# Where two engines' loop code is placed, and which engine opens the section: a streaming row-variance kernel on one Trainium2 core

## The chip, the core and the metric

The kernel runs on one core of one Trainium2 chip. The metric is the device time of one execution in microseconds (us); less is better. Of the core's engines four take part: SyncE (SP in the profile), which issues every transfer; VectorE (DVE) and ScalarE (ACT), which do the arithmetic; and GpSimd (POOL), which copies small results. TensorE (PE) runs only the barriers.

## The reference

For every row of 1,024 numbers the variance is wanted, as the mean of the squares less the square of the mean:

```python
def reference(x):                     # x: 32 x 512 x 1024, float32
    mean_sq = np.mean(x**2, axis=-1)
    sq_mean = np.mean(x, axis=-1)**2
    return (mean_sq - sq_mean).astype(np.float32)   # 32 x 512
```

There are 16,384 rows, 64 MiB in all, and each number is read once.

## The kernel before, in words

The rows are laid out as 128 partitions by 128 columns; a column is one row of 1,024 numbers in each of the 128 partitions. The columns go by in groups of eight (`GROUP`), and one load brings a group, 4 MiB, from `in_x_dram` into one of three buffers `xt0`, `xt1`, `xt2` (`NBUF`). Twelve groups go through the buffers in four turns (`TURNS`) of three. The last 32 columns are loaded by smaller and smaller transfers (`END_LOADS`: 8, 6, 6, 4, 3, 2, 1 columns, and four half columns): the first of these goes into `xt0` once more, the others into `xt_end`.

Of each group of eight, ACT takes three columns (`NACT`) and DVE five. ACT makes a column in two passes over it: `act_mean` (L104) sums it into `neg_mean`, `act_var` (L109) sums the squares of the difference. DVE makes a column with two `bn_stats` (one for each half, L100) and one `bn_aggr` (L163). What they find for a turn stands in `stage`, and POOL copies the variances from there to `mv` (L146), which is stored at the end by two transfers. The end columns are written straight to `mv` (L175 to L199 on DVE, L104 and L109 on ACT).

The order of the work is written by hand, with semaphores, inside one critical section (`tc.tile_critical`, L123), in which nothing is scheduled by a planner. `load` (L82) adds 16 to a buffer's `landed` semaphore when it has landed, one for each of 16 DMA engines. `take` (L96) waits for a semaphore and takes the same number off it again. DVE, once a buffer has landed, adds one to `go` for ACT; ACT adds one to `act_done`; and DVE's last `bn_aggr` of a group adds one to `done`, on which SP waits before it loads that buffer again. All loads stand in one queue, SP's, one after the other.

The four turns are a loop in the program of DVE (L150) and one in the program of ACT (L205), each made by `nc.Fori`. Its argument `head_slot` fixes where in the engine's program the loop's first instruction stands: at slot 128 (`HEAD`) of a block of 256 instruction slots (`FETCH_BLOCK_INSTRUCTIONS`). It does so with an alignment instruction just ahead of the loop, which the program loader turns into a branch over the padding:

```python
            self.engines[e].addr_align(
                FETCH_BLOCK_INSTRUCTIONS, offset=slot, max_nops=0
            )
        self.br(loop_start, engines=engines)
```

In the trace this branch is the compare-and-branch record of L150 on DVE and of L205 on ACT. ACT also loads its function table (L204) ahead of its loop.

Around the section stand instructions that are not in the kernel's text. First comes a barrier of all engines (L257): each adds one to a gather semaphore, POOL waits for them all and then releases all. Then the section is opened by one engine, its synchronizing engine, here SP: it adds one to a semaphore by a no-operation, and each of SP, POOL, DVE and ACT waits for that in a branch into the section. At its end the same engine, SP, adds one to a second semaphore; SP, POOL, DVE and ACT wait for it and report back, SP waits for the reports and adds once more to the first one, and SP goes on to a barrier (L268) by way of a drain that waits for this. A second barrier ends the program. With `no_gpsimd_drain=True` POOL reports by a no-operation in place of a drain.

Of the kernel before, what the change touches and what calls it, by code (L numbers as in the profile page):

```python
# [7 lines left out]


# [1 line left out]
def kernel(  # L11
# [13 lines left out]
    nc = tc.nc  # L25
# [3 lines left out]
    ENG = mybir.EngineType  # L29
# [13 lines left out]
    TURNS = 4  # L43
# [6 lines left out]
    HEAD = 128  # L50
# [14 lines left out]
    sync, act, dve, gps = nc.sync, nc.scalar, nc.vector, nc.gpsimd  # L65
# [12 lines left out]
    def load(dst, c0, n, sem, f0=0, f=D):  # L78
        b0, pitch, row0 = next(b for b in BLOCKS if b[0] <= c0 < b[0] + b[1])
        assert c0 + n <= b0 + pitch  # L80
        ap = [[pitch * D, P], [D, n], [1, f]] if n > 1 else [[pitch * D, P], [1, f]]
        sync.dma_start(  # L82
            out=dst,
            in_=dataclasses.replace(xf, offset=(row0 + c0 - b0) * D + f0, ap=ap),
        ).then_inc(sem, 16)

    def store(block):
        b0, pitch, row0 = block
        sync.dma_start(
            out=dataclasses.replace(out, offset=row0, ap=[[pitch, P], [1, pitch]]),  # L90
            in_=mv[:, 1, b0 : b0 + pitch],
        ).then_inc(stored, 16)

    def take(engine, sem, n):
        engine.wait_ge(sem, n)
        engine.sem_inc(sem, -n)  # L96

    def halves(st, xcol):
        for h in range(2):
            last = dve.bn_stats(out=st[:, h, :], in_=xcol[:, h * H : (h + 1) * H])  # L100
        return last

    def act_mean(i, xcol, nm):
        return act.activation(  # L104
            out=junk[i], in_=xcol, func=ACTF.Copy, scale=-S / D, accum_out=nm
        )

    def act_var(i, xcol, nm, var):
        return act.activation(  # L109
            out=junk_sq[i], in_=xcol, func=ACTF.Square, scale=S, bias=nm, accum_out=var  # L110
        )
# [8 lines left out]
        at += n  # L120
    assert at == ncols - IN_HALVES

    with tc.tile_critical(no_gpsimd_drain=True):  # L123

        for g in range(TURNS * NBUF):
            if g >= NBUF:
                sync.wait_ge(done, g - NBUF + 1)
            load(xt[g % NBUF], g * GROUP, GROUP, landed[g % NBUF])
        sync.wait_ge(done, TURNS * NBUF - NBUF + 1)
        load(xt[0], END0, GROUP, landed_end[0])  # L130
        c = END0 + GROUP
        for b, n in enumerate(END_LOADS[1:], 1):
            k = c - END0 - GROUP
            load(xt_end[:, k : k + n, :] if n > 1 else xt_end[:, k, :], c, n, landed_end[b])
            c += n
        b = len(END_LOADS)
        for c in range(c, ncols):
            for h in range(2):
                dst = xt_end[:, c - END0 - GROUP, h * H : (h + 1) * H]
                load(dst, c, 1, landed_end[b], h * H, H)  # L140
                b += 1

        gps.sem_inc(copied, 1)
        for t in range(TURNS):
            gps.wait_ge(done, (t + 1) * NBUF)
            gps.tensor_copy(  # L146
                out=mv[:, 1, t * PER_TURN : (t + 1) * PER_TURN], in_=stage[:, :, 1]
            ).then_inc(copied, 1)

        with nc.Fori(0, TURNS, engines=[ENG.DVE], head_slot={ENG.DVE: HEAD}):  # L150
            take(dve, copied, 1)
            for b in range(NBUF):
                take(dve, landed[b], 16)
                dve.sem_inc(go, 1)
                mine = range(b * GROUP + NACT, (b + 1) * GROUP)
                for j in mine:
                    last = halves(stats[:, j, :, :], xt[b][:, j - b * GROUP, :])
                last.then_inc(dve_step, 1)
                take(dve, dve_step, 1)
                for j in mine:  # L160
                    if j == mine[-1]:
                        take(dve, act_done, 1)
                    last = dve.bn_aggr(out=stage[:, j, :], in_=stats[:, j, :, :])  # L163
                last.then_inc(done, 1)
        n = 0
        waiting = None
        seen = -1
        for b, c, col in end_cols:
            if END_WHO[c - END0] != "D":
                continue  # L170
            if b != seen:
                dve.wait_ge(landed_end[b], 16)
                seen = b
            st = stats_end[:, c - END0, :, :]
            dve.bn_stats(out=st[:, 0, :], in_=col[:, :H])  # L175
            if waiting:
                waiting()
            n += 1
            dve.bn_stats(out=st[:, 1, :], in_=col[:, H:]).then_inc(dve_step, 1)  # L179

            def waiting(n=n, c=c, st=st):
                dve.wait_ge(dve_step, n)
                dve.bn_aggr(out=mv[:, :, c], in_=st)  # L183

        b = len(END_LOADS)
        for c in range(ncols - IN_HALVES, ncols):
            st = stats_end[:, c - END0, :, :]
            col = xt_end[:, c - END0 - GROUP, :]
            dve.wait_ge(landed_end[b], 16)
            dve.bn_stats(out=st[:, 0, :], in_=col[:, :H])  # L190
            waiting()
            dve.wait_ge(landed_end[b + 1], 16)
            n += 1
            dve.bn_stats(out=st[:, 1, :], in_=col[:, H:]).then_inc(dve_step, 1)  # L194
            b += 2

            def waiting(n=n, c=c, st=st):
                dve.wait_ge(dve_step, n)
                return dve.bn_aggr(out=mv[:, :, c], in_=st)  # L199

        waiting().then_inc(dve_step, 1)
        dve_steps = n + 1

        act.preload_act_table(ACTF.Square)  # L204
        with nc.Fori(0, TURNS, engines=[ENG.Activation], head_slot={ENG.Activation: HEAD}):  # L205
            for b in range(NBUF):
                take(act, go, 1)
                mine = range(b * GROUP, b * GROUP + NACT)
                for i, j in enumerate(mine):
                    last = act_mean(i, xt[b][:, i, :], neg_mean[:, j : j + 1])  # L210
                last.then_inc(act_step, 1)
                take(act, act_step, 1)
                for i, j in enumerate(mine):
                    last = act_var(i, xt[b][:, i, :], neg_mean[:, j : j + 1], stage[:, j, 1:2])
                last.then_inc(act_done, 1)
        n = 0
        for b in range(len(END_LOADS)):
            mine = [(c, col) for bb, c, col in end_cols if bb == b and END_WHO[c - END0] == "A"]
            if not mine:
                continue  # L220
            act.wait_ge(landed_end[b], 16)
            for i, (c, col) in enumerate(mine):
                k = c - END0
                last = act_mean(i, col, neg_mean_end[:, k : k + 1])
            n += 1
            last.then_inc(act_step, 1)
            act.wait_ge(act_step, n)
            for i, (c, col) in enumerate(mine):
                k = c - END0
                last = act_var(i, col, neg_mean_end[:, k : k + 1], mv[:, 1, c : c + 1])  # L230
            n += 1
            last.then_inc(act_step, 1)
        act_steps = n

        sync.wait_ge(copied, 1)
        store(BLOCKS[0])
        sync.wait_ge(act_step, act_steps)
        sync.wait_ge(dve_step, dve_steps)
        store(BLOCKS[1])
        sync.sem_clear(range(sems[0].num, sems[-1].num + 1))  # L240
        sync.wait_ge(stored, 32)
        sync.sem_clear(stored)
# [30 lines left out]
```

## Time and profile before

| | before |
|---|---|
| median of 3 runs (lowest to highest) | 165.64 us (165.6 to 165.7) |
| time of the profiled execution | 165.63 us |
| its span in the profile | 163.7 us, so 1.9 us lie outside |
| DVE busy | 107.0 us, 65% of the span |
| ACT busy | 107.3 us, 66% |
| POOL busy | 1.0 us, 1% |
| DMA queue q1 (the loads and stores) | 67.18 MB, 96.2% of 16 DMA engines |
| DMA queue q14 (instructions) | 2 packets, 0.02 MB |
| read from HBM | 67.11 MB, 410 GB/s over the span |

The span runs from the first to the last recorded instruction of the kernel. The share of q1 says how much of the time of all 16 DMA engines its packets filled. A busy share of an engine is a mean over the whole span; DVE and ACT have nothing to do until the first load has landed, and the profile shows their first column at 13.94 and 13.98 us.

### The profile page before, as it was taken

The numbers are of one execution on the slowest core, as the hardware profiler recorded it, in microseconds if no ns is written. First come the engines' busy times: TensorE is split into PE (matmuls) and PEld (weight loads), VectorE is DVE, ScalarE is ACT, GpSimd is POOL, SyncE is SP. The second block draws the span as 40 slices with busy tenths as digits, with TensorE's granted clock in tenths as the row PEclk, the third lists the DMA queues.
The fourth block names the chain that finished last, engine by engine and source line by source line (L and its number), as shares of the span: only waits on it lengthen the run. The fifth ranks groups of instructions, "written<-read, shape, count | busy, mean of one in ns | idle before, by whom it ended". The sixth has DMA issues, their size and how long they took to land. (4 is left out here: it accounts for less than half of the span.)

```text
span 163.7 us, 615 instructions
## 1 busy us (share of the span) xinstructions
DVE 107.0 (65%) x243; ACT 107.3 (66%) x189; POOL 1.0 (1%) x8
## 2 busy tenths in 40 slices
DVE  0005929487492957839296692948749397859993
ACT  3005939488493957939397593948849398759692
POOL 0000000000000000000000000000000000000000
DMA  6999999999998999999999989999999999999980
GB/s 204 432 400 480 400 424 472 392 488 400 408 488 384 440 456 392 480 408 400 480 400 424 472 384 464 432 400 480 400 408 488 406 396 468 396 430 412 405 297 14
DMA packets 3602, 67.19 MB, mean 411 GB/s; under 512 B 656, under 2 KB 656, under 8 KB 1296
## 3 DMA queue, kind: packets, MB, share of 16 engines
q1 hardware_dynamic: 3600, 67.18, 96.2%
q14 instruction: 2, 0.02, 0.0%
HBM read 67.11 MB, written 0.07 MB: 410 GB/s over the span
## 5 line engine op out<-in xcount | busy, mean ns | idle before, releaser
L100 DVE BATCH_NORM_STATS2 stats<-xt 128x6 f32<-128x512 f32 x120 | 72.4, 679 | 41.1 <-DVEq L96 41.1
L104 ACT ACTIVATE junk<-xt 128x1024 bf16<-128x1024 f32 x39 | 40.7, 1045 | 45.9 <-ACTq L96 43.3
L109 ACT ACTIVATE junk_sq<-xt,neg_mean 128x1024 f32<-128x1024 f32 x36 | 39.7, 1104 | 1.5
L163 DVE BATCH_NORM_AGGREGATE stage<-stats 128x2 f32<-128x12 f32 x60 | 7.6, 177 | 6.9 <-DVEq L96 5.2
L104 ACT ACTIVATE junk<-xt_end 128x1024 bf16<-128x1024 f32 x8 | 8.4, 1050 | 4.9 <-DMA xt_end<-in_x_dram 4.8
L175 DVE BATCH_NORM_STATS2 stats_end<-xt_end 128x6 f32<-128x512 f32 x14 | 9.5, 679 | 3.2 <-DMA xt_end<-in_x_dram 3.2
L109 ACT ACTIVATE junk_sq<-xt_end,neg_mean_end 128x1024 f32<-128x1024 f32 x8 | 8.9, 1113 | 0.2
L179 DVE BATCH_NORM_STATS2 stats_end<-xt_end 128x6 f32<-128x512 f32 x14 | 9.0, 640 | 0.0
L104 ACT ACTIVATION_READ_ACCUMULATOR junk<-xt 128x1 f32 x39 | 7.2, 186 | 0.0
L109 ACT ACTIVATION_READ_ACCUMULATOR junk_sq<-xt,neg_mean 128x1 f32 x36 | 6.7, 186 | 0.0
L175 DVE BATCH_NORM_STATS2 stats_end<-xt 128x6 f32<-128x512 f32 x5 | 3.4, 681 | 2.3 <-DMA xt<-in_x_dram 2.3
L183 DVE BATCH_NORM_AGGREGATE mv<-stats_end 128x2 f32<-128x12 f32 x19 | 3.7, 194 | 0.0
L109 ACT ACTIVATE junk_sq<-xt,neg_mean_end 128x1024 f32<-128x1024 f32 x3 | 3.3, 1104 | 0.0
L179 DVE BATCH_NORM_STATS2 stats_end<-xt 128x6 f32<-128x512 f32 x5 | 3.2, 648 | 0.0
L204 ACT ACT_TABLE_LOAD x1 | 1.3, 1283 | 0.9 <-SPq L123 0.9
L190 DVE BATCH_NORM_STATS2 stats_end<-xt_end 128x6 f32<-128x512 f32 x2 | 1.4, 695 | 0.4 <-DMA xt_end<-in_x_dram 0.4
L146 POOL COPY mv<-stage 128x24 f32<-128x24 f32 x4 | 0.8, 204 | 127.0 <-DVE stage L163 127.0
L109 ACT ACTIVATION_READ_ACCUMULATOR junk_sq<-xt_end,neg_mean_end 128x1 f32 x8 | 1.5, 186 | 0.0
L104 ACT ACTIVATION_READ_ACCUMULATOR junk<-xt_end 128x1 f32 x8 | 1.5, 186 | 0.0
L194 DVE BATCH_NORM_STATS2 stats_end<-xt_end 128x6 f32<-128x512 f32 x2 | 1.3, 650 | 0.0
L109 ACT ACTIVATION_READ_ACCUMULATOR junk_sq<-xt,neg_mean_end 128x1 f32 x3 | 0.6, 186 | 0.0
L199 DVE BATCH_NORM_AGGREGATE mv<-stats_end 128x2 f32<-128x12 f32 x2 | 0.4, 202 | 0.0
(4 smaller groups left out, 0.4 us busy)
## 6 DMA issues: line engine op xcount, KB each, us to landing
xt<-in_x_dram SPq DMA_DIRECT2D x13, 4096.0 KB, 21.6
xt_end<-in_x_dram SPq DMA_DIRECT2D x2, 3072.0 KB, 32.0
xt_end<-in_x_dram SPq DMA_DIRECT2D x1, 2048.0 KB, 39.8
xt_end<-in_x_dram SPq DMA_DIRECT2D x1, 1536.0 KB, 43.1
xt_end<-in_x_dram SPq DMA_DIRECT2D x1, 1024.0 KB, 45.1
xt_end<-in_x_dram SPq DMA_DIRECT2D x4, 256.0 KB, 42.0
xt_end<-in_x_dram SPq DMA_DIRECT2D x1, 512.0 KB, 45.9
out_dram<-mv SPq DMA_DIRECT2D x1, 56.0 KB, 1.6
```

The lines of the kernel that those rows point to most:

```text
L100: last = dve.bn_stats(out=st[:, h, :], in_=xcol[:, h * H : (h + 1) * H])
L104: return act.activation(out=junk[i], in_=xcol, func=ACTF.Copy, scale=-S / D, accum_out=nm)
L109: return act.activation(out=junk_sq[i], in_=xcol, func=ACTF.Square, scale=S, bias=nm, accum_out=var)
L146: gps.tensor_copy(out=mv[:, 1, t * PER_TURN : (t + 1) * PER_TURN], in_=stage[:, :, 1]).then_inc(copied, 1)
L163: last = dve.bn_aggr(out=stage[:, j, :], in_=stats[:, j, :, :])
L175: dve.bn_stats(out=st[:, 0, :], in_=col[:, :H])
L179: dve.bn_stats(out=st[:, 1, :], in_=col[:, H:]).then_inc(dve_step, 1)
L183: dve.bn_aggr(out=mv[:, :, c], in_=st)
L190: dve.bn_stats(out=st[:, 0, :], in_=col[:, :H])
L194: dve.bn_stats(out=st[:, 1, :], in_=col[:, H:]).then_inc(dve_step, 1)
L199: return dve.bn_aggr(out=mv[:, :, c], in_=st)
L204: act.preload_act_table(ACTF.Square)
```

## The change

`head_slot` is dropped from both loops. In its place the two engines get the same alignment instruction, with the same block and the same offset, ahead of the critical section, so that on DVE and ACT slot 128 is now the first instruction behind that alignment (the waiting branch into the section), and the loops follow a few slots later. The section's synchronizing engine is now GpSimd (`ENG.Pool`) and not SP, so the opening no-operation, the collection of the reports and the closing no-operation are POOL's.

```diff
+from concourse.bass_core_rust import FETCH_BLOCK_INSTRUCTIONS
...
-    with tc.tile_critical(no_gpsimd_drain=True):
+    for engine in (act, dve):
+        engine.addr_align(FETCH_BLOCK_INSTRUCTIONS, offset=HEAD, max_nops=0)
+
+    with tc.tile_critical(sync_engine=ENG.Pool, no_gpsimd_drain=True):
...
-        with nc.Fori(0, TURNS, engines=[ENG.DVE], head_slot={ENG.DVE: HEAD}):
+        with nc.Fori(0, TURNS, engines=[ENG.DVE]):
...
-        with nc.Fori(0, TURNS, engines=[ENG.Activation], head_slot={ENG.Activation: HEAD}):
+        with nc.Fori(0, TURNS, engines=[ENG.Activation]):
```

No transfer, no arithmetic instruction and no semaphore inside the section is changed. The lines of the changed kernel stand one to four further down than those of the kernel before.

## The prediction

> **What bounds the kernel now.** I read the shares first: DVE and ACT are busy 65% and 66%, the load queue 96.2%. The chain of waits then says what ended last (share of the span; DMA, engine or SP's queue, and line):
>
> ```profile
> DMA 28%; DVE 2%; SPq 2%; issue 0%
> ...
> DMA xt_end<-in_x_dram 28%; SPq L82 2%; DVE stats_end L190 1%; DVE stats_end L194 1%; DVE mv L199 0%; DVE stage L163 0%; DVE mv L183 0%
> ```
>
> It reaches back only to 108 us, where the last loads are issued; before that the DMA row of the slices is full from the second slice on, so the transfers set the pace throughout. What an edit outside the loops can move is the beginning, the end, and anything that shares the DMA engines. The timeline's first microseconds (start, duration, engine, line):
>
> ```profile
> 0.34 0.10 POOL L257 MEMSET const-uint8-127<- 128x1 uint8 x1
> 0.91 1.28 ACT L204 ACT_TABLE_LOAD   x1 [0.91 <-SPq L123]
> 0.94 1.34 SPq L82 DMA_DIRECT2D xt<-in_x_dram  x3
> 13.94 2.47 DVE L100 BATCH_NORM_STATS2 stats<-xt 128x6 f32<-128x512 f32 x4 [13.94 <-DVEq L96]
> ```
>
> The first load is issued at 0.94 us, after the opening by SP (L123). DVE computes nothing for 13 us more. The DMA view of two windows, 2 to 3 us and 3.5 to 4.5 us (queue: packets, MB, share of 16 engines), shows what else is on the DMA engines:
>
> ```profile
> q1 hardware_dynamic: 13, 0.43, 145.8%
> q14 instruction: 1, 0.01, 4.3%
> ```
>
> ```profile
> q1 hardware_dynamic: 16, 0.52, 124.5%
> q14 instruction: 1, 0.01, 1.9%
> ```
>
> Two instruction fetches fall into the load stream. 4.3% and 1.9% of 16 engine-microseconds are 0.69 and 0.30 us. The packet records give them in full: 8,192 bytes each, from 2.134 us (0.688) and from 3.911 us (0.307); the first data packets start at 1.975 us. Elsewhere in the span this queue has nothing.
>
> The landing records have 16 increments for each load, one a DMA engine. For the first load 15 come between 12.58 and 13.12 us, the last at 13.71. For the last load 15 come between 158.79 and 159.29, the last at 159.90. So one DMA engine is late by 0.59 to 0.61 us from beginning to end, never catching up, and every wait for a load waits for it. A 32,768-byte packet takes a DMA engine 1.21 us in the steady stream, so 8,192 bytes are a quarter of that, 0.30 us, and two fetches are 0.61 us: the lateness. On the late engine the packet starts fit as well: a data packet starts at 2.819, as the first fetch ends (2.134 + 0.688 = 2.822), another at 4.214, as the second ends (4.218). I read it so: both fetches went to one DMA engine, inside the stream, and the whole kernel runs behind that engine.
>
> The end (timeline of DVE):
>
> ```profile
> 157.96 0.69 DVE L190 BATCH_NORM_STATS2 stats_end<-xt_end 128x6 f32<-128x512 f32 x1 [0.36 <-DMA xt_end<-in_x_dram]
> ...
> 160.67 0.21 DVE L199 BATCH_NORM_AGGREGATE mv<-stats_end 128x2 f32<-128x12 f32 x1
> ```
>
> DVE restarts at 157.96, 0.03 us after a landing at 157.93, and follows landings to the last at 159.90. ACT's last run starts at 156.00 from a landing at 155.97. Both tails move with the landings, unchanged in length.
>
> **The change part by part.**
>
> *Start of the loads.* Before, SP passes the barrier at 0.656, does its opening no-operation at 0.721, the branch that waits for it at 0.791, and issues at 0.944. Afterwards POOL opens: it releases the barrier at 0.614, its next instruction can follow after the 0.077 us between its two barrier records (0.691), and an engine sees it 0.036 us later (SP's no-operation at 0.721, ACT's branch at 0.757). SP branches at about 0.73 in place of 0.791: 0.06 us earlier. This alone moves 15 of the DMA engines.
>
> *The fetches.* Before, the alignment branch runs at 1.001 us on ACT and at 1.048 on DVE, behind the wait for the section, the register move and, on ACT, the issue of the table load. Afterwards it follows the barrier directly, at about 0.66 + 0.065 (SP's step from 0.656 to 0.721): 0.725 on ACT, 0.73 on DVE, 0.28 and 0.32 us earlier. If these branches bring on the fetches, which first show 1.1 us after them, the first starts near 1.83 in place of 2.134, and the loads at 1.975 - 0.06 = 1.91. The late DMA engine then begins its work, the same bytes, about 0.30 us earlier, and ends that much earlier: I take 0.30 us, by the shift of the branch. Bounds: at worst the late engine gains only the 0.06 of the loads (fetches not moved); at best both are through before its data come, and it falls in with the others: 0.59 + 0.06 = 0.65 us.
>
> One rule speaks against any gain here. The Trainium skill, "Runtime: NRT & Kernel Launch", section "Instruction fetch mechanics", has the sequencer fetch ahead of itself, with the cost of crossing a block mostly hidden. For DVE's and ACT's own time the trace agrees, since they wait until 13.9 us; for the DMA engine that carries the fetch it does not, by the 0.6 us lateness. By the page alone this term would be 0.06 us and the total about 165.4 us.
>
> A second one offers another cause of the late engine: "DMA: Bandwidth & Descriptors", section "Latency and other measured facts", finds two of the sixteen engines usually slower. The lateness here is as large at 13 us as at 159, so it is one event at the start and no lower rate. By that page the lateness would stay, and the total again be about 165.4 us.
>
> *What the fetches' cover hides.* DVE's alignment branch takes 0.545 us to its next instruction (1.048 to 1.593). It now comes ahead of the section's wait; with the 0.20 us of that branch (0.778 to 0.980) and the move DVE is at its loop by about 1.55 us, ACT's table load runs from about 1.4 to 2.7. Both then wait for the first landing, 13 us away; without that cover the branch would cost 0.55 us. The loops start two slots further on; their back edge (0.42 us on DVE, three times) falls into idle time: DVE sits 41.1 us ahead of its loop's statistics, ACT 43.3. I cost these edits at nothing.
>
> *The end of the section.* Before, from SP's last clear at 162.551: SP signals at 162.610, POOL answers at 162.652, SP drains at 162.689, collects at 162.763 and 162.822, signals again at 162.888, drains at 162.963 and 163.026, and POOL passes the barrier at 163.058: 0.507 us. Afterwards POOL has signalled the end long before, after its fourth copy, and SP drains where it signalled, at 162.610. Two chains follow. SP's own instructions are two collecting waits and two drains; with the steps they had before (0.074, 0.059, 0.066 and 0.063) SP reports to the barrier at 162.872 and POOL passes 0.032 later, at 162.904. POOL's answer, for which SP's first of these drains waits, comes in time: POOL sees SP's report 0.042 later (162.652), does its closing no-operation after 0.077 (162.729), seen after 0.04 at 162.77, where SP drains at 162.809. So the path is shorter by 163.058 - 162.904 = 0.15 us: one signal of SP's own and one no-operation less. Behind POOL's new waits nothing of its own is queued but the barrier. Bounds: if POOL's three steps took twice as long each, SP's drain would come at 162.93 and 0.03 us would be left; if SP's barrier report followed POOL's answer directly (162.77 + 0.063 + 0.032), it would be 0.19.
>
> *The sum.* 0.30 + 0.15 = 0.45 us (the 0.06 of the loads is inside the 0.30, since the late engine sets the end). The profiled execution took 165.63 us (span 163.7 and 1.9 around it); 165.63 - 0.45 = 165.18, and against the median of 165.64 the same: **165.2 us**, 0.3% less. Bounds: 0.06 + 0.03 = 0.09 (165.5), and 0.65 + 0.19 = 0.84 (164.8).
>
> **The rivals.** *The fetches leave the stream altogether.* Both come together near 1.83, and the late engine's data only after them; a later start of data on some DMA engines (first packets from 1.975 to 2.53 on the others) leaves room. Then the next-latest engine sets the end: 0.65 + 0.15 = 0.80, 164.8 us. Against it: one fetch alone took 0.69 us, two reach 2.4 or later.
>
> *The fetches stay where they are.* They may belong to an engine whose branch doesn't move, since the records don't name the owner. For it: the second comes 2.9 us after the branches. Against it: just two engines branch over padding, just two fetches follow. Then 0.06 + 0.15 = 0.21, 165.4 us, no difference that can be told: about 0.2%, 0.33 us, is what a measurement of this kernel can tell from no change.
>
> *Slower: the end of DVE's program crosses into code that isn't loaded.* Counted from the loop's head at slot 128, DVE's last barrier instruction is at slot 256, the first of the next block; two slots are now pushed in ahead of the loop, so three instructions of the closing barriers lie beyond. If that block had to be fetched then, all engines would wait in the barrier for as long as from a branch to the end of the fetch at the start (1.048 to 2.822): 1.77 - 0.45 = 1.3 us slower, 166.9 us. Against it: DVE's last instruction before ran at 163.623, with SP's at 163.613 and no fetch near; the block was there. It decides only if the block is no longer loaded ahead.
>
> **How the numbers follow.** Forecast 0.45, fetches clear of the stream 0.28, fetches stay 0.18, slower 0.09. Faster by over 0.2% (under 165.31 us): all of the second and most of the first, which has it where its saving passes 0.33, 0.66 together. Within 0.2%: the third and the rest of the first, 0.25. Slower: 0.09. The range runs from 164.7 to 165.5: the bounds of the sum with 0.1 below for the scatter of the runs (165.6 to 165.7); it takes in two rivals and leaves the slow case out.
>
> **What would show it.** First load issue at 0.88 us in place of 0.94; the alignment branches near 0.73; instruction packets starting at or before 1.9 us; the gap between the last and the last but one landing of each load below 0.59, at about 0.35; the last landing near 159.6; span near 163.2; 0.35 us from SP's clear to POOL's barrier in place of 0.51. I am wrong if the gap stays at 0.6, if it vanishes, or if a fetch turns up in the closing barriers.

## The result, and the profile after

The changed kernel takes 165.14 us (median of 8 runs, 164.98 to 165.47) beside 165.61 for the kernel before on the same chip (8 runs, 165.56 to 165.87). The ratio is 0.9971, with a 95% interval of 0.996 to 0.9982: 0.3% faster, 0.47 us. 165.2 was forecast. Run once more, beside the last experiments, it gave 0.9973 (0.9964 to 0.9982).

The profiled execution took 165.27 us, with a span of 163.5 (163.48 in the trace) and 1.79 us around it; the one of before took 165.63, with 163.68 and 1.95. The timeline's first microseconds after:

```profile
0.34 0.10 POOL L261 MEMSET const-uint8-127<- 128x1 uint8 x1
0.89 2.46 SPq L83 DMA_DIRECT2D xt<-in_x_dram  x3
1.31 1.28 ACT L208 ACT_TABLE_LOAD   x1 [1.31 <-PEq L261]
13.49 3.07 DVE L101 BATCH_NORM_STATS2 stats<-xt 128x6 f32<-128x512 f32 x5 [13.49 <-DVEq L97]
```

The first load is issued 0.06 us earlier, the table load 0.40 us later and still under cover, and DVE's first column comes 0.45 us earlier. The DMA view of the window from 1 to 2 us (queue: packets, MB, share of 16 engines):

```profile
q1 hardware_dynamic: 5, 0.16, 57.8%
q14 instruction: 2, 0.02, 10.6%
```

Both instruction packets now start there. The packet records have them from 1.768 (0.405 us long) and from 1.922 (1.289), beside first data packets from 1.902. No instruction packet is left between 3.5 and 4.5 us. In the landing records the last increment of the first load comes at 13.27, the last but one at 12.90; of the last load at 159.43 and 159.12. So the late DMA engine stands 0.36 us behind the next at the first load and 0.31 at the last, where it was 0.60 at both, and the last landing is 0.47 us earlier. The tail follows it (timeline of DVE):

```profile
159.57 0.64 DVE L198 BATCH_NORM_STATS2 stats_end<-xt_end 128x6 f32<-128x512 f32 x1
160.25 0.21 DVE L203 BATCH_NORM_AGGREGATE mv<-stats_end 128x2 f32<-128x12 f32 x1
```

In the closing something new shows. These are the waits of SP's queue in the barriers (line waited at, releaser: us in total, times, longest), of the kernel before and then of the changed one:

```profile
SPq L268 <- PEq L268: 0.5, 2, 0.4
```

```profile
SPq L246 <- DMA out_dram<-mv: 1.1, 1, 1.1
SPq L272 <- PEq L272: 0.9, 2, 0.7
```

One barrier wait has grown from 0.4 to 0.7 us (the L246 line, SP's wait for the last store, is needed further down). The view names PE's queue, but PE's drain had come at 162.772; by the instruction records the late one is DVE. Its drain ahead of the second barrier starts at 163.155, 0.535 us after the instruction in front of it (162.620); before, that step was 0.110 (163.189 to 163.299). POOL passes the two closing barriers 0.811 us apart in place of 0.435. The packet records have one more instruction packet of 8,192 bytes in each trace, behind the end of the span: it starts at 164.809 before and at 163.821 after.

The ledger of the two profiled executions, in the order of time:

| piece | before | after | difference |
|---|---|---|---|
| last landing | 159.898 | 159.430 | -0.468 |
| from there to SP's last clear | 2.653 | 2.697 | +0.044 |
| from there to POOL's first closing barrier | 0.507 | 0.362 | -0.145 |
| first to second closing barrier | 0.435 | 0.811 | +0.376 |
| from there to the end of the span | 0.182 | 0.183 | +0.001 |
| outside the span | 1.955 | 1.787 | -0.168 |
| time | 165.63 | 165.27 | -0.36 |

The 0.044 is DVE's: its last `bn_stats` starts 0.14 us after the last landing where it was 0.10, because it follows the half column before, whose landing moved by 0.43 only (159.26 to 158.83).

### The profile page after: what moved, and what is told of

Read it like the earlier page. It is cut to its first block, busy times and chain, and to the rows that moved or that the text cites. A ratio compares the mean times of both kernels' runs of the same rounds, so it can differ in the third digit from the quotient of the medians.

```text
span 163.5 us, 617 instructions
## 1 busy us (share of the span) xinstructions
DVE 107.0 (65%) x243; ACT 107.3 (66%) x189; POOL 1.0 (1%) x8
```

## The experiments

Three theories are told apart. F: the alignment branches bring on the two fetches, and a fetch that meets the load stream makes a DMA engine late for good. P, its rival: the gain is GpSimd's opening and closing alone, and one DMA engine is late by nature. C: DVE's late step in the closing is the price of going on into the next block of its program. Later texts add R, that what the second fetch costs is decided by a race with the first data, and its rival N, that it is fixed. Lateness is how far the last of a load's 16 increments comes behind the last but one; where two DMA engines are late together it shows little. Each run's lateness and packets are those of its one profiled execution.

**Alignment alone, and GpSimd alone.** `e1_align_only` takes `sync_engine=ENG.Pool` out of the changed kernel. `e2_pool_only` puts it into the kernel before:

```diff
-    with tc.tile_critical(no_gpsimd_drain=True):
+    with tc.tile_critical(sync_engine=ENG.Pool, no_gpsimd_drain=True):
```

> Alignment ahead of the section as in the changed kernel, but SP stays the synchronizing engine. Theory F (fetches): the alignment branches bring on the two instruction fetches, which delay one DMA engine. Then both fetches start near 1.8 us as in the changed kernel (1.77 and 1.92), the first load is issued at 0.94, the last landing of each load is 0.3 to 0.4 us behind the last but one (0.60 before, 0.37 after), the last landing comes near 159.45 (159.90 before), the path from SP's clear to the first closing barrier stays 0.51 us, and DVE is late by about 0.4 us in the second closing barrier as in the changed kernel: about 165.3 to 165.4 us. Rival P (all of it is GpSimd's opening and closing; one DMA engine is late by its nature): lateness 0.60, 165.6 us, as before.

Measured: 165.44 us, ratio 0.9982 (0.9973 to 0.9991). The fetches start at 1.764 and 1.927, the first load is issued at 0.944, lateness is 0.31 to 0.35, the last landing comes at 159.50. SP's clear to the first barrier takes 0.507 us, the two barriers are 0.813 apart. All as F has it; P's 0.60 is out.

> GpSimd as the synchronizing engine, alignment at the loops as before. Theory F: first load at 0.88 us in place of 0.94, fetches still near 2.1 and 3.9 us, lateness 0.6 us, last landing 159.84, 0.15 us less at the end, no late DVE in the closing barriers: 165.4 us. Rival P: 165.1 us, the whole gain of the changed kernel.

Measured: 165.47 us, ratio 0.9988 (0.9979 to 0.9997). Start (0.887), SP's clear to the barrier (0.363) and the step between the barriers (0.434) are as expected. The fetches are not where I expected them: they start at 4.111 and 4.983, while the branches ran at 0.990 and 1.049 as before. The window from 4 to 5.5 us:

```profile
q1 hardware_dynamic: 20, 0.66, 104.3%
q14 instruction: 2, 0.02, 2.6%
```

The loads come 0.06 us earlier here, and each fetch starts only as a data packet of its engine ends (4.112 and 4.987). And now two DMA engines are late: the first load's last increments are 13.56 and 13.61, the third last 12.97. So the two fetches run on two DMA engines, one each. The packet records show the toll: a data packet takes 1.21 us in this stretch, but the one behind the first fetch (4.111 to 4.418) takes 1.46, the one behind the second (4.983 to 5.292) 1.75. A fetch costs its engine its own 0.31 us and 0.25 to 0.53 more on the packet behind it. Each edit alone gains about 0.2 us, and P falls. The times alone would not part the alignment's gain from the whole (the intervals of `e1_align_only` and the changed kernel overlap); that GpSimd adds its part is read from the traces, 0.363 us to the barrier in place of 0.507.

**Other places for the code.** `e3_slot96` has `offset=HEAD - 32`; `e4_no_align` leaves the alignment out.

> The changed kernel with the alignment's offset at 96 in place of 128, so that everything on DVE and ACT stands 32 slots earlier and DVE's closing barrier instructions end near slot 226 and not behind slot 256. Theory F with the crossing: fetches and lateness as in the changed kernel (0.37 us), but DVE is not late in the second closing barrier: its step between the barriers falls from 0.81 to 0.44 us, and the time from 165.1 to between 164.75 and 165.0. Rival (DVE's late drain has another cause, such as the engine's own pipeline): 0.81 us stays, 165.1.

Measured: 165.31 us, ratio 0.9976 (0.9966 to 0.9987). The step between the barriers is 0.434, as C has it, with 1.78 us outside the span. But the gain was not had, because the fetches moved. The first three microseconds are clean; they come at 27.179 and 37.723 (windows from 27 to 28 and from 37 to 38 us):

```profile
q1 hardware_dynamic: 8, 0.26, 64.4%
q14 instruction: 1, 0.01, 1.9%
```

```profile
q1 hardware_dynamic: 14, 0.46, 106.1%
q14 instruction: 1, 0.01, 1.9%
```

The loops begin at slot 98 here, so their first turn passes slot 128, the middle of a block, and the fetches come in that turn. Up to the second load the last increment is 0.03 to 0.05 us behind the last but one; in the load that lands after the first fetch it is 0.9 us behind, and after the second the last but one has moved by 0.3 too. Behind the fetch at 27.179 the next packet takes 1.81 us: 0.31 + 0.60 = 0.91, the jump in the landings. The last landing is 160.14.

> GpSimd as the synchronizing engine and no alignment at all on DVE and ACT, so that no branch over padding runs. Theory F: no fetch in the first 5 us, lateness near 0 in all loads unless a fetch comes later in the stream; last landing near 159.25; 164.8 us, or a fetch in the middle of the stream and 165.1. Rival (the fetches come with the start of the program and not with the branches): two fetches as before, lateness 0.4 to 0.6, 165.1 to 165.4.

Measured: 165.38 us, ratio 0.9981 (0.9972 to 0.999). No fetch in the first 5 us, and four loads long lateness is 0.02 to 0.06 us: no single DMA engine stands 0.6 us back by nature (the last two together are 0.10 to 0.15 behind the third, which nothing here explains). Then fetches come at 44.053 and 128.820, and the last increment falls 0.73 us behind the last but one after the first of them. The time is that of a kernel with a late engine. The two fetches can be moved, but no run here is without them.

**The race at the start.** `e7_wait10` is the changed kernel with SP held back by ten increments of an unused semaphore ahead of its first load:

```diff
+        for _ in range(10):
+            sync.sem_inc(pad, 1)
         for g in range(TURNS * NBUF):
```

> The changed kernel with ten semaphore increments on SP ahead of the first load, about 0.65 us. Theory R: both fetches are through before any data, lateness 0 to 0.05 us in all loads, last landing 159.43 - 0.36 + 0.65 = 159.7, 165.4 us. Rival N: lateness 0.36 stays, last landing 160.1, 165.8 us.

Measured: 165.88 us, ratio 1.0005 (0.9996 to 1.0014). The first load is issued at 1.522. In the window from 1 to 2 us the fetches have the DMA engines for themselves:

```profile
q14 instruction: 2, 0.02, 5.7%
```

They are through at 2.40, the first data packet starts at 2.54. Lateness is 0.10 to 0.13 (0.05 was expected; the first packets of the 16 engines are spread from 2.54 to 3.46), the last landing is 160.04. By lateness R holds; the time and the last landing are near those that N had named (165.8 and 160.1; the kernel before took 165.82 on this chip), for the wait costs more than it brings.

`e8_dve_only` aligns DVE alone.

> The changed kernel with the alignment on DVE alone; ACT stands where the compiler puts it. Theory F, one fetch an aligning engine: one fetch in the first 5 us, DVE's, near 1.9 us, with 0.3 to 0.4 us of lateness if it is DVE's that races with the data; ACT's comes in the middle of the stream, where it adds 0.3 to 0.7 us on its DMA engine (either fetch in the middle of the stream did so in the kernel without alignment): 165.3 to 165.5 us. Rival (both fetches belong to one engine): two fetches at the start and none later, 165.1 us.

Measured: 165.41 us, ratio 0.9978 (0.9969 to 0.9988). One fetch at 1.925, the other at 128.755, where the last increment goes from 0.04 to 0.42 us behind the last but one. So each aligning engine brings one fetch, and the second of the changed kernel's is DVE's. My 0.3 to 0.4 us for it at the start was a miss: it met the data and lateness was 0.02 to 0.04. What this meeting costs is not fixed: 0.03 in the first load here, 0.17 and 0.36 in two profiles of the changed kernel.

**The closing step.** `e5_shorter` takes six instructions out of DVE's program, so that its recorded end lies ahead of slot 256. ACT gets a column more, and `go` rides on a `bn_stats`:

```diff
-    END_WHO = "AAADDDDD" "AADDDD" ...
+    END_WHO = "AAADDDDD" "AAADDD" ...
...
-                dve.sem_inc(go, 1)
...
+                    if j == mine[0]:
+                        first.then_inc(go, 1)
```

> The changed kernel with six instructions fewer in DVE's program, placed as before: the go signal rides on the group's first bn_stats, and one column of the second end load goes from DVE to ACT, so that DVE's last barrier instruction falls from slot 258 to slot 252. Theory C (crossing slot 256 costs DVE about 0.4 us in the closing barriers): the step between the two closing barriers falls from 0.81 to 0.43 us, fetches stay at 1.77 and 1.92, lateness at about 0.36, time 164.8 to 164.95. Rival (the crossing is only moved behind the span): the step falls but the time outside the span grows from 1.79 to about 1.95, 165.0.

Measured: 165.23 us, ratio 0.9957 (0.9945 to 0.9969). The step between the barriers is 0.434, but 2.06 us lie outside the span, 0.27 more than in the changed kernel: the rival is right, the price has moved behind the span. Lateness was 0.40 to 0.47 in this profile.

`e6_shorter_wait3` adds three increments on SP.

> The kernel of the last text with three semaphore increments on SP ahead of the first load, about 0.2 us. Theory R (race: the late DMA engine is late because its fetch comes in at the same time as the first data): the first data packets come near 2.1, the second fetch at 1.92 is through before them, lateness falls from 0.36 to under 0.1; the last landing is 0.36 - 0.2 = about 0.15 us earlier, 164.65 to 164.8 us. Rival N (a DMA engine late by its nature, or by the fetch's own work, which stays the same): lateness 0.36, everything 0.2 us later, 165.1 us.

Measured: 164.93 us, ratio 0.9948 (0.9935 to 0.9961). The first load is issued at 1.112, the first data packet starts at 2.13, and lateness is 0.01 to 0.04 us. The last landing is 159.44, as in the changed kernel: what the wait costs the lateness gives back. The time outside is 2.08. N falls, but R's picture is not what the trace shows either: the second fetch starts at 2.186 (2.481 in `e5_shorter`), behind the first data and not ahead of them. Over all profiles that have both fetches at the start, the later one to end did so between 2.39 and 2.56 us where lateness was at most 0.17, and between 2.92 and 3.21 where it was 0.08 to 0.47 (the runs that follow included). What decides how long a fetch takes there is open.

`e9_plus2` shifts DVE's code the other way, two slots later:

```diff
-    for engine in (act, dve):
-        engine.addr_align(FETCH_BLOCK_INSTRUCTIONS, offset=HEAD, max_nops=0)
+    for engine, slot in ((act, HEAD), (dve, HEAD + 2)):
+        engine.addr_align(FETCH_BLOCK_INSTRUCTIONS, offset=slot, max_nops=0)
```

> The changed kernel with the alignment's offset on DVE at 130 in place of 128: two slots later, so that DVE reaches slot 256 with the drain behind its last bn_aggr and not with the first closing barrier. Theory C2 (the first step into a new block costs DVE about 0.45 us wherever it comes, and nothing where DVE waits anyway): DVE is idle from 160.6 to 162.6 us there, so the step between the closing barriers is 0.43 us (0.81 in the changed kernel) and the time outside the span stays at 1.79; lateness 0.36 as there; 0.3 to 0.4 us less than the changed kernel, 164.8 us. Rival (the cost is bound to the closing barriers, or is moved behind the span as in the shortened kernel): step 0.81, or outside 2.05; time as the changed kernel.

Measured: 164.9 us, ratio 0.9948 (0.9934 to 0.9961), while the changed kernel beside it has 0.9973 (0.9964 to 0.9982). SP's barrier waits are back where they were before the change, while its wait for the last store has grown from 1.1 to 1.3 us:

```profile
SPq L246 <- DMA out_dram<-mv: 1.3, 1, 1.3
...
SPq L272 <- PEq L272: 0.5, 2, 0.4
```

The late step is still in the trace, but earlier: from DVE's first drain at 160.094 to its next at 160.858 are 0.764 us (0.341 in the changed kernel), while DVE has nothing to do until 162.627. The barriers are 0.434 apart, and 1.787 us lie outside. C is shown in its second form: the step costs DVE 0.42 us in the barriers and here, and the barriers nothing where DVE waits anyway. But the step is followed by a fetch. Where DVE's program goes past slot 256 the packet records have a third instruction packet (`e3_slot96`, which ends ahead of it, has none). It starts 0.66 us behind the late drain in the changed kernel, after the end of the span, and 0.66 us behind it here: at 161.513, for 0.380 us, among the last store's packets (161.226 to 161.561). That it moved with DVE's two slots marks it as DVE's. The store's last increment comes 0.17 us after the one before it, and SP's last clear 1.75 us after the store's issue, 1.57 to 1.59 in every other profile. So some 0.17 us of the gain was paid back in this execution; on the other side lateness was 0.08 to 0.13 as well, so 0.1 to 0.2 us of what it gained may be the race.

`e10_plus2_wait3` and `e11_plus2_wait2` add three and two increments on SP.

> The kernel of the last text and the three increments on SP ahead of the first load (0.23 us, as tried). Theories C2 and R together: lateness under 0.05, step 0.43, outside 1.79: 164.6 to 164.7 us, the fastest. Rival: 164.9, as the shortened kernel with the three increments.

> As before, with two increments (about 0.15 us). Theory R: lateness stays small (under 0.15) if the data packets still come behind the second fetch, and 0.07 us are won against three: 164.55 to 164.7. If the second fetch then meets the data, lateness 0.2 to 0.4 and 164.7 to 164.9.

Measured: 164.85 us (ratio 0.9944, 0.9931 to 0.9958) and 164.83 us (0.9953, 0.9939 to 0.9966), lateness 0.13 to 0.17 and 0.02 to 0.04 (in the second, two DMA engines are late together, 0.15 behind the third). Their third fetches start at 161.99 and 161.85, 0.94 and 0.90 us behind the late drain and behind the store's packets, and the store is not late. The 164.6 I had put down was too low by 0.2: the wait costs what it saves. These two and `e9_plus2` can't be told apart. All three beat the kernel before, and the intervals of `e9_plus2` and `e10_plus2_wait3` lie clear below the changed kernel's as well; `e9_plus2` does it with one number changed.

`e12_changed_again` is the changed kernel itself.

> The changed kernel once more, beside these three on the same chip. All theories: 0.3% faster than the kernel before, about 165.15 us; lateness between 0 and 0.4 us by the race of the second fetch with the data, step 0.81.

Measured: 165.3 us, ratio 0.9973 (0.9964 to 0.9982), runs from 165.03 to 165.56; lateness 0.15 to 0.19, barriers 0.812 apart.

## Why the prediction was right, and where it was not

*The direction and the size* stand: 0.3% less was forecast, 0.29% measured. That the size came out so near is in part luck: one term of the sum was too small and another was missing, each by about 0.2 us, and they cancelled.

*The start of the loads* is right: 0.887 us, 0.88 forecast. *The branches* ran at 0.735 and 0.762 (0.725 and 0.73), and the fetches followed 1.03 and 1.16 us behind them; that the branches bring them on is shown by the kernel without alignment and by the one that aligns DVE alone.

*Both fetches on one DMA engine, 2 x 0.30 us* was wrong. They are on two engines, as the two late engines of `e2_pool_only` show. The fit to 0.61 was chance: in the trace of before the data packet behind the first fetch (from 2.819) ends at 4.290 with the others, and the late engine has the second fetch alone, 0.307 us, and the packet behind it, from 4.214, takes 1.75 us in place of 1.21. That is 0.85, and the last increment is 0.84 us behind the middle of the 16. I had compared it with the next-latest engine alone, and so found the number I looked for.

*The saving of 0.30 us at the last landing* was mis-sized; it was 0.47 in the profile shown. Of this 0.29 is lateness (0.60 to 0.31 in the last load), and 0.18 that the next-latest engine ran earlier (159.29 to 159.12). In the second profile of the changed kernel the last landing is 159.29, so 0.61 was saved. The term is no fixed shift, since what the second fetch costs at the start differs from one execution to the next, and the bounds of 0.06 to 0.65 described it better than the value.

*The end of the section* is right: 0.362 us from SP's clear to the barrier, 0.35 forecast.

*The edits costed at nothing* hold for the loops and for the table load, and fail for the two slots ahead of them. The rival that had DVE's end beyond slot 256 named the place, but put the price at a whole fetch (1.77 us) or nothing. It is neither: the block was there, and the step into it still took 0.42 us more, 0.38 of which stood in the barriers' way. In the kernel before I had read the unhurried last instruction at 163.623 as proof that nothing was lost. Counted by the trace's records (60 of a turn, 68 behind the loop) that instruction stands at slot 255, one less than I had counted, and the late drain of the changed kernel and of `e9_plus2` at 256: the step came behind the last record. The third instruction packet says so too: it starts 1.19 us after 163.623 before, and 1.20 us after the record ahead of the late drain (162.620) in the changed kernel. 0.17 us of the step's price show there (1.955 us outside, against 1.78 to 1.79 wherever DVE's code stood otherwise, the shortened kernels excepted). So the change paid 0.38 inside and saved 0.17 outside, a term of 0.21 that the sum lacked, and the span came to 163.48 where 163.2 was forecast. The saving at the landings, larger by 0.17 than the 0.30 put down, about made up for it (0.36 us less in the two profiled executions, 0.47 by the medians), which no part of the working had foreseen.

On the rule of the Trainium skill that spoke against a gain ("Runtime: NRT & Kernel Launch", "Instruction fetch mechanics": the cost of crossing a block is mostly hidden), the runs show both sides. The engine that runs the code was not seen to wait for a fetch: in the changed kernel DVE goes on at 1.332, ahead of its fetch at 1.922, and the late drain at 163.155 is ahead of the packet at 163.821. But the DMA engine that carried a fetch lost 0.56 to 0.92 us in the stream, and the time followed that DMA engine.

The other cause that was offered, two DMA engines that are usually slower, plays no part in the 0.6 us: in the first four loads of `e4_no_align` the last engine stands 0.02 to 0.06 us behind the next. The page's row ("DMA: Bandwidth & Descriptors", "Latency and other measured facts") puts it down, as a best guess, to descriptors made by software, which the prediction left out; the loads here go by the queue q1 `hardware_dynamic`.

## What to carry to other kernels

In a kernel that the DMA engines bound, look at the landings of one load engine by engine, and at every packet that is not data: one small fetch in a full stream makes its DMA engine late for the rest of the kernel. Code placement decides when such fetches come, so let an engine enter its last blocks before the stream begins, or while it waits, and look where the fetch that follows falls: in `e9_plus2` it met the last store. Count the slots to the last barrier, too: two instructions more ahead of a loop can move a step into a stretch for which all engines wait.

## What the hardware showed that was not expected

- A fetch of 8,192 bytes takes a busy DMA engine 0.31 us, and the 32,768-byte packet behind it 1.46 to 1.83 us in place of 1.21 in the full stream. Why the packet is stretched is open.
- Where the alignment branches to slot 128 or 130 ran 0.12 us or more ahead of the first load's issue, their fetches followed after 1.03 to 1.17 us, and later only for DVE's in the two shortened kernels (1.42 and 1.72). Where they ran 0.06 to 0.16 us behind it, the fetches followed after 1.1 and 2.9 us (before) and after 3.1 and 3.9 (`e2_pool_only`). These are single profiles, and why it is so is open.
- DVE's step into the next block of its program cost 0.42 us though the next instruction packet started only 0.66 to 0.94 us after it, about as much as DVE's back edge (0.42) and less than its alignment branch (0.55 to 0.57).
